# A SwiGLU block with Strassen's seven products for two of three token blocks, and the down projection in its own phase

## The chip, the cores and the metric

The kernel runs on one core of one Trainium2 chip. The metric is the device time of one execution in microseconds (us). PE is the matrix engine (PEld its weight loads), DVE the vector engine, ACT the scalar engine, POOL the GpSimd engine, SP the engine whose queue issues most transfers.

## The reference, cut to what matters

One decoder layer for 1024 prompt tokens and 32 sample tokens, in float32. The change touches the stretch from the memory attention's output projection to the end:

```python
x = layer_norm(DEEPNORM_ALPHA * x + memory_attention(x, mem_k, mem_v, w_mem_q, w_mem_o), ln2_g, ln2_b)
ffn = (jax.nn.silu(x @ w_gate) * (x @ w_up)) @ w_down      # w_gate, w_up 1024 x 2816, w_down 2816 x 1024
x = layer_norm(DEEPNORM_ALPHA * x + ffn, ln3_g, ln3_b)
```

## The kernel before

Activations lie with features on the 128 partitions and tokens along the free dimension, in three blocks of 384, 384 and 288 tokens (0, 1 and 2). Every float32 operand of PE is split in two rounded parts, high (a cast by ACT) and low (value minus high, by DVE). A product of a 128x128 weight tile and a block is three matmuls (`mm3`, L205 to L207): high by high, high weight by low value, low weight by high value.

Weights come as a stream of strips of 128x1024 (512 KB): a DMA issued from ACT's queue into `wraw` (two buffers), the cast to `whi` (L186), the subtraction to `wlo` (L187), four buffers of each. `gemm` goes through groups of four strips, inside them block by block; a strip is released behind block 2, which starts the split of a later one. All instructions are given out in program order, and a scheduler with a cost model decides the order in each engine's queue; every queue is then worked off strictly in that order.

The mem output projection (strips 50 to 57) adds its results to the residual `z` (L767, DVE) and sums the features on POOL (L777). Behind the last strip of a block its layer norm (`norm`) is put on a list and advanced step by step beside later products: a ones-matmul on PE sums over partitions (L788), ACT copies the mean (L791), the subtraction goes half to DVE and half to POOL (L796), ACT squares (L800) into the two `sq` buffers, DVE adds (L809 to L812), a second ones-matmul (L813), an inverse root (L443 to L446), a multiplication by DVE (L820), gain and bias feature by feature in turn on ACT and POOL (L826, L824), and the split of the result (L829, L830) into `a0h`, `a0l` (features 0 to 3) and `a1h`, `a1l` (4 to 7).

The feed-forward part takes the 22 feature tiles of the hidden dimension in chunks of 4 (the last of 2). A chunk is its gate and up strips, the gated values (`evac_gu`: silu by ACT L922, product by DVE L931, split L933 and L934) in SBUF, and the down strips. The last chunk goes block by block, so that the final norm of one block runs beside the products of the next; block 2's takes the short way (`fine`, L796 to L806).

Of the kernel before, what the change touches and what calls it, by code (L numbers as in the profile page):

```python
# [13 lines left out]
OP = mybir.AluOpType  # L14
# [28 lines left out]
def _weight_stream(i):  # L43
# [92 lines left out]
# ---------------------------------------------------------------- kernel  # L136
class Body:
# [4 lines left out]
    # ---- small helpers  # L142
# [66 lines left out]
    # groups: list of strip groups; x(b, k) -> (hi, lo) APs; evac(n, b, ps)  # L209
    def gemm(self, base, nstrips, x, evac, kt=8, blocks=(0, 1, 2), group=4):  # L210
# [26 lines left out]
    def body(self, st):  # L237
# [3 lines left out]
        self.limit = 50  # L241
# [15 lines left out]
    def phase12(self, st):  # L257
# [13 lines left out]
        self.s_x1 = scr("s_x1", [128, 8 * T])  # L271
        self.qs = self.t(self.cp, [128, 4, 32], "qs")
# [7 lines left out]
    def project(self, A, xa, og):  # L280
        tc, nc, a = self.tc, self.nc, self.a

        # queries: the tokens of each tile in the order of their residue mod 4
# [31 lines left out]
        with tc.tile_pool(name="ps_a", bufs=1, space=PSUM) as self.pp2, tc.tile_pool(name="ssm_small", bufs=1) as self.sp, tc.tile_pool(name="ssm_part", bufs=1) as sh, \  # L315
# [21 lines left out]
            # g_att and g_ssm: the factors that the sums of squares over 1024 instead of 512 and the doubled y leave  # L337
# [54 lines left out]
    def gemm_v(self, base, nch, lhs, rows, evac, release=True):  # L392
        # lhs(r, k) -> (hi, lo) stationary APs of row tile r
# [46 lines left out]
    # ---- -2/sqrt(ps + eps), ps [128, n] in PSUM  # L440
# [8 lines left out]
    # ---- sums of squares over features, for the rms norms  # L449
# [51 lines left out]
    # ---- residual and the recurrent half of the output projection  # L501
# [25 lines left out]
    # ---- windowed attention: prompt heads, with the sample batches as filler  # L527
# [22 lines left out]
    def attention(self):  # L550
# [7 lines left out]
        # a query tile meets its own and the previous key tile in full, and in the older ones the keys of its residue  # L558
        # mod 4 only; scores are laid out as [older tiles, 32 keys each | previous tile | own tile]
# [23 lines left out]
        def trans(h, qt):  # L583
# [13 lines left out]
            if qt and not e:  # L597
                # the key tile that is far from the odd tile of the pair only
# [3 lines left out]
        # two query tiles at a time; in the columns of a residue they meet the same older tiles  # L602
        def pv(hp, q0):
# [7 lines left out]
            # the own keys of the even tile are the previous ones of the odd tile  # L611
# [44 lines left out]
    # the first head pair, kept until its half of the mixer is free  # L656
# [12 lines left out]
    # ---- windowed attention of the sample batches, four at a time on the column groups of the array  # L669
# [93 lines left out]
    # ---- residual + layer norm of one block; z [128, 8, n] holds the residual and then the result  # L763
# [7 lines left out]
    # sums over the feature tiles: the first ones on GpSimd, those from cut on on VectorE  # L771
# [573 lines left out]
```

## Time and profile before

| | |
|---|---|
| time, three runs | 1746.70, 1746.38, 1744.56 us, median 1746.38 |
| span of the profiled execution | 1744.7 us, 1.7 us under the median of the runs |
| busy, share of the span | PE 94%, DVE 45%, ACT 29%, POOL 19% |

The span runs from the first to the last recorded instruction or transfer; what lies around it is the 1.7 us. A recorded matmul overlaps the next one, so PE's pitch is read from the starts of matmuls that follow each other. The granted clock stands as a share of full speed: 1.00 is 2.4 GHz and 0.5 is 1.2 GHz.

### The profile page before, as it was taken

To read this page: it belongs to the slowest core of one execution; us is meant where nothing else is said; L and a number is where in the kernel's file an instruction comes from. 1 tells how busy PE (TensorE), PEld (TensorE's weight loads), DVE (VectorE), ACT (ScalarE), POOL (GpSimd) and SP (SyncE) were. 2 spreads that over 40 slices of the span, in tenths; PEclk is the share of its full clock that TensorE was granted. 3 is DMA by queue.
4 is the path that set the end of the run, shared out by engine and by line. 5 is a ranking of instruction groups with operands and counts; after the bars stand their busy time and mean duration, and the time that the engine had idled before them with its cause. 6 is when DMAs were issued, how large, how long until landed. Compare 5 with 4: busy or idle time off the path is not lost.

```text
span 1744.7 us, 27141 instructions
## 1 busy us (share of the span) xinstructions
PE 1644.6 (94%) x11150; PEld 1505.1 (86%) x11150; DVE 793.4 (45%) x1614; ACT 506.5 (29%) x990; POOL 324.9 (19%) x372
## 2 busy tenths in 40 slices
PE   7797998999999988999998999999999999999996
PEld 7786785666766978987898999999999999999995
DVE  7564482177554985245427623223223322322347
ACT  5221121176334254245304520121121121121124
POOL 3403412032222644002126400000000000000025
PEclk9899999999999989999999999999999999999998
DMA  7435777813422366136610111111111111111102
GB/s 269 118 77 137 204 207 156 291 57 118 142 73 95 113 198 210 49 121 216 223 49 26 35 48 39 49 49 49 49 49 49 49 49 49 49 49 49 49 0 100
DMA packets 89052, 174.77 MB, mean 100 GB/s; under 512 B 12832, under 2 KB 48160, under 8 KB 88160
## 3 DMA queue, kind: packets, MB, share of 16 engines
q1 hardware_dynamic: 71072, 108.02, 20.6%
q10 hardware_dynamic: 17856, 65.02, 11.1%
q8 instruction: 88, 1.44, 0.3%
q14 instruction: 36, 0.29, 0.1%
HBM read 139.86 MB, written 33.14 MB: 99 GB/s over the span
## 4 chain that ended last, share of the span: by engine, by line
PE 79%; DVE 9%; DMA 5%; ACT 2%; SPq 2%; POOL 2%; issue 1%; ACTq 0%; POOLq 0%; DVEq 0%
PE g L205 21%; PE g L207 21%; PE g L206 21%; PE s L568 2%; PE s L570 2%; DVE wlo L187 1%; PE g L592 1%; PE q L743 1%; DMA wraw<-in_wst_dram 1%; POOL z L824 1%; DMA skv<-in_cv_dram 1%; DMA skv<-in_ckT_dram 1%; DVE z L820 1%; PE g L403 1%; PE g L404 1%
## 5 line engine op out<-in xcount | busy, mean ns | idle before, releaser
L205 PE MATMUL g<-a0h,whi 128*128 128x384 f32 (+1 forms) x1008 | 331.6, 331 | 12.4 <-ACT whi L186 7.6
L206 PE MATMUL g<-a0l,whi 128*128 128x384 f32 (+1 forms) x1008 | 330.0, 327 | 3.5 <-DVE a0l L830 3.5
L207 PE MATMUL g<-a0h,wlo 128*128 128x384 f32 (+1 forms) x1008 | 329.5, 327 | 2.3 <-DVE wlo L187 2.2
L205 PE MATMUL g<-a1h,whi 128*128 128x384 f32 (+1 forms) x960 | 312.2, 326 | 0.8 <-ACT a1h L328 0.8
L206 PE MATMUL g<-a1l,whi 128*128 128x384 f32 (+1 forms) x960 | 309.9, 323 | 2.0 <-DVE a1l L330 1.8
L207 PE MATMUL g<-a1h,wlo 128*128 128x384 f32 (+1 forms) x960 | 309.8, 323 | 0.0
L186 ACT CAST whi<-wraw 128x1024 fp32r<-128x1024 f32 x122 | 127.9, 1049 | 413.7 <-PE g L206 355.8
L187 DVE TENSOR_TENSOR wlo<-wraw,whi 128x1024 fp32r<-128x1024 f32 x122 | 162.6, 1334 | 117.0 <-ACT whi L186 116.8
L205 PEld LDWEIGHTS g<-a0h,whi 128*128 128x128 f32 x1008 | 192.5, 191 | 18.6 <-ACT whi L186 7.6
L206 PEld LDWEIGHTS g<-a0l,whi 128*128 128x128 f32 x1008 | 193.2, 192 | 5.6 <-DVE a0l L830 4.1
L207 PEld LDWEIGHTS g<-a0h,wlo 128*128 128x128 f32 x1008 | 193.1, 192 | 4.8 <-DVE wlo L187 3.3
L205 PEld LDWEIGHTS g<-a1h,whi 128*128 128x128 f32 x960 | 181.3, 189 | 6.1 <-issue 3.1
L206 PEld LDWEIGHTS g<-a1l,whi 128*128 128x128 f32 x960 | 181.4, 189 | 2.9 <-DVE a1l L330 2.0
L207 PEld LDWEIGHTS g<-a1h,wlo 128*128 128x128 f32 x960 | 181.5, 189 | 1.2 <-issue 1.1
L931 DVE TENSOR_TENSOR sil<-sil,g 128x384 f32<-128x384 f32 (+1 forms) x66 | 34.4, 521 | 268.6 <-PE g L207 266.8
L205 PE MATMUL g<-hh,whi 128*128 128x384 f32 (+1 forms) x480 | 154.2, 321 | 0.0
L206 PE MATMUL g<-hl,whi 128*128 128x384 f32 (+1 forms) x480 | 154.1, 321 | 0.0
L207 PE MATMUL g<-hh,wlo 128*128 128x384 f32 (+1 forms) x480 | 154.0, 321 | 0.0
L777 POOL TENSOR_TENSOR acc<-z 128x384 f32<-128x384 f32 (+1 forms) x9 | 9.8, 1085 | 738.0 <-DVE z L769 691.2
L769 DVE TENSOR_TENSOR z<-z,g 128x384 f32<-128x384 f32 (+1 forms) x120 | 61.4, 518 | 109.2 <-PE g L207 109.1
L207 PEld LDWEIGHTS g<-hh,wlo 128*128 128x128 f32 x480 | 90.2, 188 | 0.0
L206 PEld LDWEIGHTS g<-hl,whi 128*128 128x128 f32 x480 | 90.1, 188 | 0.0
(371 smaller groups left out, 2509.2 us busy)
## 6 DMA issues: line engine op xcount, KB each, us to landing
wraw<-in_wst_dram ACTq DMA_DIRECT2D x124, 512.0 KB, 3.4
skv<-in_ckT_dram SPq DMA_DIRECT2D x40, 256.0 KB, 4.5
skv<-in_cv_dram SPq DMA_DIRECT2D x40, 256.0 KB, 4.9
kvm<-in_cmk_dram SPq DMA_DIRECT2D x16, 512.0 KB, 5.0
wraw<-in_cmv_dram SPq DMA_DIRECT2D x16, 512.0 KB, 4.4
out_dram<-stg SPq DMA_DIRECT2D x32, 128.0 KB, 4.0
zt<-in_xT_dram SPq DMA_DIRECT2D x8, 384.0 KB, 3.5
s_z<-zt SPq DMA_DIRECT2D x8, 384.0 KB, 2.3
```

The source lines that it names most:

```text
L186: self.nc.scalar.copy(h[:], r[:])
L187: self.nc.vector.tensor_tensor(out=l[:], in0=r[:], in1=h[:], op=OP.subtract)
L205: mm(out, wh, xh, start=start, stop=False)
L206: mm(out, wh, xl, start=False, stop=False)
L207: mm(out, wl, xh, start=False, stop=stop)
L403: mm(ps[:, :256], xh, wh, start=k == 0, stop=False)
L404: mm(ps[:, :256], xh, wl, start=False, stop=False)
L568: mm(ps[:, 32 * nf:w], q, k[:, 128 * max(qt - 1, 0):128 * qt + 128], start=True, stop=True)
L570: mm(ps[32 * r:32 * r + 32, 0:32 * nf], q[:, 32 * r:32 * r + 32], k[:, 0:128 * nf].rearrange("p (i r) -> p r i", r=4)[:, r], start=True, s ...
L592: nc.tensor.transpose(ps[:, 128 * x:128 * x + 128], S[:, c:c + 128], self.ident[:])
L769: self.nc.vector.tensor_tensor(out=z[:, k], in0=z[:, k], in1=ps[:, :n], op=OP.add)
L931: v.tensor_tensor(out=hf[:, :n], in0=hf[:, :n], in1=ps[:, :n], op=OP.mult)
```

## The change

For blocks 0 and 1 the gate and up products of a feature tile are seen as a 2x2 product: weight halves a11, a12 (gate, input features 0 to 3 and 4 to 7) and a21, a22 (up), value halves b11, b21 (block 0) and b12, b22 (block 1). Instead of eight products of halves there are Strassen's seven, m1 to m7, each of 12 matmuls of 384 columns. Sums of values (`combine`) are formed once, behind the norms; sums of weights are formed for each feature tile on POOL. Nine half strips for each tile are split by ACT and DVE. Block 2 keeps direct products. The gated values go to DRAM (`s_h`) and come back in `down`, a phase of its own in chunks of 4, 4, 4, 4, 2 and 4. The mem output projection does strips 0 to 3 for blocks 0 and 1, strips 4 to 7 for all, and strips 0 to 3 once more, loaded and split again, for block 2. Strips of gate and up are loaded through SP's queue, the gate strip into `wraw`, the up strip into `wru` of a pool `up` that is opened where the pool `ln3` of the norms was closed.

```diff
-CHUNKS = [(0, 4), (4, 4), (8, 4), (12, 4), (16, 4), (20, 2)]
+NF = 22
+DOWN = [(0, 4), (4, 4), (8, 4), (12, 4), (16, 2), (18, 4)]
+MO, GU = 50, 58
+DN = GU + 2 * NF
...
-                    if b == 2:
+                    if b == rel:
                         self.release(base + s)
...
+        self.rows = list(range(MO + 8)) + list(range(MO, MO + 4)) + list(range(DN, a["wst"].shape[0]))
+        self.s_h = scr("s_h", [128, NF * T])
...
-        with tc.tile_pool(name="z2", bufs=1) as zp, tc.tile_pool(name="ln3", bufs=1) as self.lp, \
-                tc.tile_pool(name="ffn", bufs=1) as fp:
+        with tc.tile_pool(name="z2", bufs=1) as zp:
             z = self.load_z(zp, self.s_x1)
-            self.gemm_n(50, 8, xs, self.post_ln(z, x, 28, 36))
-            self.advance(99)
...
+            with tc.tile_pool(name="xc", bufs=1) as xp:
+                with tc.tile_pool(name="ln3", bufs=1) as self.lp:
+                    X = self.mem_out(z, xp, x, xs)
+                with tc.tile_pool(name="up", bufs=1) as up:
+                    self.gate_up(up, X, x[2])
+            with tc.tile_pool(name="ln4", bufs=1) as self.lp, tc.tile_pool(name="ffn", bufs=1) as fp:
+                self.down(z, fp)
...
+    def mem_out(self, z, xp, x, xs):
...
+            self.todo.append(self.norm(z[b], acc[b], 28, 36, x[b] if b == 2 else None))
+            if b == 0:
+                self.todo.append(self.combine(X, xp, z, ("m4", "m2")))
+            if b == 1:
+                self.todo.append(self.combine(X, xp, z, ("m3", "m5", "m1", "m6", "m7")))
+        X = {}
+        self.gemm_n(MO, 4, xs, lambda n, b, ps: evac(n, b, ps), blocks=(0, 1), rel=1)
+        self.gemm_n(MO + 4, 4, xs, lambda n, b, ps: evac(n + 4, b, ps))
+        self.gemm_n(MO + 8, 4, xs, lambda n, b, ps: evac(n, b, ps), blocks=(2,))
+        self.advance(99)
+        return X
...
+    def combine(self, X, xp, z, names):
+        nc = self.nc
+        part = lambda i: z[i % 2][:, 4 * (i // 2):4 * (i // 2) + 4]
+        b11, b12, b21, b22 = (part(i) for i in range(4))
+        recipe = {"m4": (b21, b11, OP.subtract, "a", 0), "m2": (b11, None, None, "a", 0),
+                  "m3": (b12, b22, OP.subtract, "a", 1), "m5": (b22, None, None, "a", 1),
+                  "m1": (b11, b22, OP.add, "1", 0), "m6": (b11, b12, OP.add, "6", 0), "m7": (b21, b22, OP.add, "7", 0)}
+        for n in names:
...
+                src = self.t(self.lp, [128, 4, 384], "sq", bufs=2)[:]
+                (nc.gpsimd if n in ("m6", "m7") else nc.vector).tensor_tensor(out=src, in0=p, in1=q, op=op)
...
+            nc.scalar.copy(hi[:], src)
+            nc.vector.tensor_tensor(out=lo[:], in0=src, in1=hi[:], op=OP.subtract)
...
+    def gate_up(self, up, X, x2):
...
+            raws[f] = [self.t(self.wp, [128, 1024], "wraw", bufs=2), self.t(up, [128, 1024], "wru", bufs=2)]
+            for i, r in enumerate(raws[f]):
+                nc.sync.dma_start(r[:], a["wst"][GU + 2 * f + i])
+        names = ("a22", "a11", "m2", "m5", "m1", "m6", "m7", "a12", "a21")
...
+                src = self.t(up, [128, 512], "wt", bufs=3)[:]
+                g.tensor_tensor(out=src, in0=q[p_], in1=q[q_], op=op)
+            t_ = self.t(self.wp, [128, 2, 512], "whi" if n in ("a22", "a11") else "wlo", F32R, 4)
+            act.copy(t_[:, 0], src)
+            v.tensor_tensor(out=t_[:, 1], in0=src, in1=t_[:, 0], op=OP.subtract)
...
+        raw(0)
+        for i in range(4):
+            unit(i)
...
+            product(p4, 384, U("a22"), *X["m4"])
+            act.copy(e4, p4[:, :384])
+            step()
+            product(p3, 384, U("a11"), *X["m3"])
+            act.copy(e3, p3[:, :384])
+            step()
+            product(p4, 384, U("m2"), *X["m2"], first=False)
+            g.tensor_tensor(out=e3, in0=e3, in1=e4, op=OP.add)
+            tt(out=d, in0=e3, in1=p4[:, :384], op=OP.subtract)
+            step()
+            product(p3, 384, U("m5"), *X["m5"], first=False)
+            tt(out=e3, in0=e3, in1=p3[:, :384], op=OP.subtract)
+            act.activation(s2, p3[:, :384], AF.Silu)
+            step()
...
+            product(p1, 384, U("m1"), *X["m1"])
+            act.copy(e1, p1[:, :384])
+            g.tensor_tensor(out=e1, in0=e1, in1=d, op=OP.add)
+            step()
+            product(p6, 384, U("m6"), *X["m6"])
+            tt(out=e1, in0=e1, in1=p6[:, :384], op=OP.add)
+            g.tensor_tensor(out=s2, in0=s2, in1=e1, op=OP.mult)
+            put(s2, f, 1)
+            step()
+            product(p1, 384, U("m7"), *X["m7"], first=False)
+            tt(out=e3, in0=e3, in1=p1[:, :384], op=OP.add)
+            act.activation(e3, e3, AF.Silu)
+            tt(out=e3, in0=e3, in1=p4[:, :384], op=OP.mult)
+            put(e3, f, 0)
+            step()
...
+            product(pg, n, U("a11"), *x2[0])
+            product(pg, n, U("a12"), *x2[1], first=False)
...
+            product(pu, n, U("a21"), *x2[0])
+            product(pu, n, U("a22"), *x2[1], first=False)
+            tt(out=sil[:, :n], in0=sil[:, :n], in1=pu[:, :n], op=OP.mult)
+            put(sil, f, 2)
...
+    def down(self, z, fp):
...
+                r = self.t(fp, [128, 4, 384], "hr", bufs=2)[:, :nf, :n]
+                nc.sync.dma_start(r, self.s_h[:, NF * off + f0 * n:NF * off + (f0 + nf) * n]
...
+                nc.scalar.copy(H[b][0], r)
+                nc.vector.tensor_tensor(out=H[b][1], in0=r, in1=H[b][0], op=OP.subtract)
...
+            for bs in ((0,), (1,), (2,)) if last else ((0, 1, 2),):
+                self.gemm_n(base, nf, lambda b, k: tuple(t_[:, k, :] for t_ in H[b]), evac_d, kt=nf, blocks=bs)
```

Line numbers move by 5 or 6 in the helpers (the norm's subtraction is L802, its multiplication L826); the new lines are L956 and L963, L964 (`combine`), L978 (strip loads), L995 to L998 (`unit`) and L1005 (`product`).

The order on DVE around the end of the mem output projection, before; z_1669 is block 1, sq_9705 holds block 2's squares, and `sil` and `hl` belong to the first feed-forward chunk:

```order
L820 TENSOR_TENSOR z_1669_8914<-z_1669_8914,rs_y_9603 128x1536 x2
L809 TENSOR_TENSOR sq_9705<-sq_9705 128x2x288
L931 TENSOR_TENSOR sil_9760<-sil_9760,g_9762 128x384
L809 TENSOR_TENSOR sq_9708<-sq_9708 128x2x288
L830 TENSOR_TENSOR a0l_1718_9524<-z_1669_8914,a0h_1717_9523 128x1536
L811 TENSOR_TENSOR sq_9705<-sq_9705,sq_9708 128x2x288
L931 TENSOR_TENSOR sil_9817<-sil_9817,g_9819 128x384
L934 TENSOR_TENSOR hl_1759_9788<-sil_9760,hh_1758_9787 128x384
L812 TENSOR_TENSOR sq_9705<-sq_9705 128x288
L934 TENSOR_TENSOR hl_1759_9788<-sil_9817,hh_1758_9787 128x384
L444 TENSOR_TENSOR rs_q_9716<-rs_y_9715 128x288
L445 SCALAR_TENSOR_TENSOR rs_q_9716<-s_9703,rs_q_9716 128x288
```

The same place after the change; z_1668 is block 0, x1, x6, x7, a0 and a1 are the operands of m1, m6, m7, m3 and m5, and sq_9724 holds block 2's squares:

```order
L826 TENSOR_TENSOR z_1669_8909<-z_1669_8909,rs_y_9494 128x1536 x2
L956 TENSOR_TENSOR sq_9543<-z_1669_8909 128x1536
L956 TENSOR_TENSOR sq_9584<-z_1668_8908,z_1669_8909 128x1536
L964 TENSOR_TENSOR a1l_1737_9581<-z_1669_8909,a1h_1736_9580 128x1536
L964 TENSOR_TENSOR a0l_1735_9577<-sq_9543,a0h_1734_9576 128x1536
L964 TENSOR_TENSOR x1l_9618<-sq_9584,x1h_9617 128x1536
L964 TENSOR_TENSOR x6l_9624<-sq_9621,x6h_9623 128x1536
L815 TENSOR_TENSOR sq_9724<-sq_9724 128x2x288
L964 TENSOR_TENSOR x7l_9657<-sq_9654,x7h_9656 128x1536
L815 TENSOR_TENSOR sq_9727<-sq_9727 128x2x288
L817 TENSOR_TENSOR sq_9724<-sq_9724,sq_9727 128x2x288
L818 TENSOR_TENSOR sq_9724<-sq_9724 128x288
```

Where work of the first chunk stood between the steps of block 2's norm, seven long subtractions and sums of `combine` now stand between block 1's multiplication and block 2's sums of squares.

PE after the change, at the end of the mem output projection (g_9687 is its last product, s_9722 the sum of block 2's squares, g_9782 the first Strassen product, m4):

```order
L209 MATMUL g_9687<-a1l_1322_7661,whi_9586 128x288
L210 MATMUL g_9687<-a1h_1321_7660,wlo_9587 128x288
L819 MATMUL s_9448<-sq_9450,ones_70 128x384
L794 MATMUL s_9718<-acc_9484,ones_70 128x288
L819 MATMUL s_9722<-sq_9724,ones_70 128x288
L1005 MATMUL g_9782<-a0h_1708_9383,whi_9766 128x384
L1005 MATMUL g_9782<-a0l_1709_9384,whi_9766 128x384
```

No product stands between the ones-matmuls and the first Strassen product.

SP's queue after the change, with the waits of each transfer, from the load of the residual on:

```order
L860 DMA z_1670_8910<-s_x_96 128x2304 [waits DMAHW7_49]
L978 DMA wraw_9758<-in_wst_dram 128x1024 [waits DMAHW3_49,DMAHW2_49,DMAHW4_49,DMAHW1_49,DMAHW6_49,DMAHW0_49,DVE_49]
L978 DMA wraw_9762<-in_wst_dram 128x1024 [waits DMAHW5_49,DMAHW3_49,DMAHW7_49,DMAHW1_49,DVE_49]
L978 DMA wru_9759<-in_wst_dram 128x1024 [waits DVE_49,Activation_49,Pool_49]
L978 DMA wru_9763<-in_wst_dram 128x1024
L978 DMA wraw_9895<-in_wst_dram 128x1024 [waits DMAHW0_49,DVE_49,Pool_49]
```

The first load of an up strip (`wru_9759`) waits for DVE, ACT and POOL, that is for the last users of the closed pool whose space it takes; block 2's multiplication, the last reader of `rs_y`, is among them. The third gate strip (`wraw_9895`) waits for readers of the first.

The end of DVE's queue before; z_1669 is block 1, z_1670 block 2, and L804, L805 are block 2's sums of squares:

```order
L820 TENSOR_TENSOR z_1669_8914<-z_1669_8914,rs_y_15673 128x768 x2
L796 TENSOR_TENSOR z_1670_8915<-z_1670_8915,s_15732 128x576 x4
L804 TENSOR_TENSOR sq_15737<-sq_15737 128x2x288
L805 TENSOR_TENSOR sq_15737<-sq_15737 128x288
L804 TENSOR_TENSOR sq_15742<-sq_15742 128x2x288
L805 TENSOR_TENSOR sq_15742<-sq_15742 128x288
L820 TENSOR_TENSOR z_1669_8914<-z_1669_8914,rs_y_15673 128x768 x2
L444 TENSOR_TENSOR rs_q_15753<-rs_y_15752 128x288
L445 SCALAR_TENSOR_TENSOR rs_q_15753<-s_15735,rs_q_15753 128x288
L446 SCALAR_TENSOR_TENSOR rs_y_15752<-rs_q_15753,rs_y_15752 128x288
L820 TENSOR_TENSOR z_1670_8915<-z_1670_8915,rs_y_15752 128x576 x4
```

And after:

```order
L802 TENSOR_TENSOR z_1670_8910<-z_1670_8910,s_16446 128x576 x4
L451 SCALAR_TENSOR_TENSOR rs_q_16350<-s_16306,rs_q_16350 128x384
L810 TENSOR_TENSOR sq_16451<-sq_16451 128x2x288
L452 SCALAR_TENSOR_TENSOR rs_y_16349<-rs_q_16350,rs_y_16349 128x384
L810 TENSOR_TENSOR sq_16456<-sq_16456 128x2x288
L811 TENSOR_TENSOR sq_16451<-sq_16451 128x288
L826 TENSOR_TENSOR z_1669_8909<-z_1669_8909,rs_y_16349 128x768 x4
L811 TENSOR_TENSOR sq_16456<-sq_16456 128x288
L450 TENSOR_TENSOR rs_q_16467<-rs_y_16466 128x288
L451 SCALAR_TENSOR_TENSOR rs_q_16467<-s_16449,rs_q_16467 128x288
L452 SCALAR_TENSOR_TENSOR rs_y_16466<-rs_q_16467,rs_y_16466 128x288
L826 TENSOR_TENSOR z_1670_8910<-z_1670_8910,rs_y_16466 128x576 x4
```

Two of block 1's multiplications stood ahead of block 2's sums and two behind them; now all four, and the last step of block 1's inverse root (L451, L452), stand ahead of the last sum of block 2 (`sq_16456`, L811).

## Rows read from the trace of the kernel before

**Rows 1.** First lines of the page: span, busy time of each engine.
```profile
span 1744.7 us, 27141 instructions
...
PE 1644.6 (94%) x11150; PEld 1505.1 (86%) x11150; DVE 793.4 (45%) x1614; ACT 506.5 (29%) x990; POOL 324.9 (19%) x372
```

**Rows 2.** Busy time of each engine in stretches of the span (start:end, length, then engines).
```profile
770.00:850.00 80.00, 71.91 (x637) 57.64 (x637) 46.29 (x180) 44.34 (x145) 18.84 (x40) 1.00 0.61 205
860.00:950.00 90.00, 86.09 (x534) 84.55 (x533) 39.83 (x46) 20.76 (x24) 35.40 (x26) 1.00 0.19 67
950.00:1000.00 50.00, 45.58 (x252) 44.14 (x251) 34.87 (x33) 24.91 (x34) 23.39 (x14) 0.93 0.07 22
1000.00:1700.00 700.00, 700.00 (x4356) 699.21 (x4355) 210.46 (x324) 121.67 (x185) 8.58 (x6) 1.00 0.14 46
...
1723.40:1744.70 21.30, 4.26 (x11) 1.62 (x9) 14.81 (x25) 8.32 (x13) 8.46 (x9) 0.62 0.33 129
```

**Rows 3.** Timeline of PE, one strip of the gate product, block 0.
```profile
1115.79 0.33 PE L205 MATMUL g<-a0h,whi 128*128 128x384 f32 x1
...
1117.87 0.33 PE L205 MATMUL g<-a1h,whi 128*128 128x384 f32 x1
```

**Rows 4.** Groups of DVE by line and shape, 860 to 1000 us.
```profile
L796 DVE TENSOR_TENSOR z<-z,s 128x1536 f32<-128x1536 f32 x2 | 3.5, 1748 | 1.7 <-ACT mean L791 1.7
L820 DVE TENSOR_TENSOR z<-z,rs_y 128x1152 f32<-128x1152 f32 x2 | 2.6, 1354 | 0.0
...
L809 DVE TENSOR_TENSOR sq<-sq 128x576 f32<-128x576 f32 x2 | 1.5, 750 | 0.0
...
L444 DVE TENSOR_TENSOR rs_q<-rs_y 128x288 f32<-128x288 f32 x1 | 0.5, 457 | 2.3 <-ACT rs_y L443 2.3
```

**Rows 5.** The same for POOL.
```profile
L796 POOL TENSOR_TENSOR z<-z,mean 128x1152 f32<-128x1152 f32 x1 | 2.7, 2690 | 5.0 <-ACT mean L791 5.0
L777 POOL TENSOR_TENSOR acc<-z 128x384 f32<-128x384 f32 x2 | 2.0, 1012 | 27.9 <-DVE z L767 27.9
L777 POOL TENSOR_TENSOR acc<-z 128x288 f32<-128x288 f32 x1 | 0.8, 802 | 5.2 <-DVE z L767 5.2
```

**Rows 6.** The same for ACT.
```profile
L829 ACT CAST a0h<-z 128x1536 fp32r<-128x1536 f32 x2 | 2.9, 1472 | 6.4 <-POOL z L824 6.4
...
L800 ACT ACTIVATE sq<-z 128x1152 f32<-128x1152 f32 x2 | 2.2, 1160 | 0.0
L933 ACT CAST hh<-sil 128x384 fp32r<-128x384 f32 x4 | 2.0, 507 | 1.3 <-DVE sil L931 1.3
```

**Rows 7.** Timeline of norms of blocks 0 and 1, three places.
```profile
918.62 1.00 POOL L777 TENSOR_TENSOR acc<-acc,z 128x384 f32<-128x384 f32 x1 [3.08 <-DVE z L767]
...
920.29 3.53 POOL L796 TENSOR_TENSOR z<-z,mean 128x1536 f32<-128x1536 f32 x1 [0.68 <-ACT mean L791]
...
942.70 3.58 POOL L824 TENSOR_SCALAR z<-z,vneg,vecs 128x384 f32<-128x384 f32 x4
...
952.97 4.20 POOL L830 TENSOR_TENSOR a1l<-z,a1h 128x1536 fp32r<-128x1536 f32 x1
...
953.75 4.50 DVE L187 TENSOR_TENSOR wlo<-wraw,whi 128x1024 fp32r<-128x1024 f32 x1
```

**Rows 8.** DMA issues of the page: size, median us from issue to landing.
```profile
wraw<-in_wst_dram ACTq DMA_DIRECT2D x124, 512.0 KB, 3.4
...
kvm<-in_cmk_dram SPq DMA_DIRECT2D x16, 512.0 KB, 5.0
...
s_x<-z SPq DMA_DIRECT2D x4, 768.0 KB, 5.0
```

**Rows 9.** Timeline of the last 21 us.
```profile
1731.95 0.46 DVE L805 TENSOR_TENSOR sq<-sq 128x288 f32<-128x288 f32 x1
1732.32 1.82 DVE L820 TENSOR_TENSOR z<-z,rs_y 128x768 f32<-128x768 f32 x2
...
1734.77 0.46 DVE L444 TENSOR_TENSOR rs_q<-rs_y 128x288 f32<-128x288 f32 x1 [0.63 <-ACT rs_y L443]
```

More of the change, by code (lines that the diff above doesn't have):

```diff
@@ L49, in _weight_stream @@
     g, u, d = _strips(i["w_gate"][0]), _strips(i["w_up"][0]), i["w_down"][0]
-    for f0, nf in CHUNKS:
-        for f in range(f0, f0 + nf):
-            out += [g[f:f + 1], u[f:f + 1]]
+    for f in range(NF):
+        out += [g[f:f + 1], u[f:f + 1]]
+    for f0, nf in DOWN:
         out.append(_pairs(d[f0 * 128:(f0 + nf) * 128]))
@@ new lines, in rest, with evac @@
+            with tc.tile_pool(name="xc", bufs=1) as xp:
[6 more added lines that the diff above has]
+    def mem_out(self, z, xp, x, xs):
+        acc, seen = [[], [], []], [[], [], []]
+        def evac(n, b, ps):
+            self.add_block(z[b], n, ps, True)
+            at = seen[b]
+            at.append(n)
+            if len(at) > 1:
+                if len(at) == 2:
+                    acc[b].append(self.t(self.lp, [128, 384], "acc", bufs=3)[:, :BLK[b][1]])
+                self.nc.gpsimd.tensor_tensor(out=acc[b][0], in0=z[b][:, at[0]] if len(at) == 2 else acc[b][0],
+                                             in1=z[b][:, n], op=OP.add)
+            if len(at) < 8:
+                self.advance(3)
+                return
+            if b == 2:
+                x[b] = self.blk_pair(b)
+            self.todo.append(self.norm(z[b], acc[b], 28, 36, x[b] if b == 2 else None))
[9 more added lines that the diff above has]
+        return X
@@ new lines, in down, with evac_d @@
+    def down(self, z, fp):
+        tc, nc, a = self.tc, self.nc, self.a
+        base = MO + 12
+        self.prefetch(999, 4)
+        for ci, (f0, nf) in enumerate(DOWN):
+            H, acc = {}, {}
+            last = ci == len(DOWN) - 1
+            for b, (off, n) in enumerate(BLK):
+                r = self.t(fp, [128, 4, 384], "hr", bufs=2)[:, :nf, :n]
+                nc.sync.dma_start(r, self.s_h[:, NF * off + f0 * n:NF * off + (f0 + nf) * n]
+                                  .rearrange("p (k n) -> p k n", n=n))
+                H[b] = [self.t(self.ap_, [128, 4, n], f"a{ci % 2}{p}{b}", F32R)[:, :nf] for p in "hl"]
+                nc.scalar.copy(H[b][0], r)
+                nc.vector.tensor_tensor(out=H[b][1], in0=r, in1=H[b][0], op=OP.subtract)
+            def evac_d(n, b, ps):
+                self.add_block(z[b], n, ps, ci == 0)
+                if not last:
+                    return
+                if n == 0:
+                    acc[b] = []
+                self.sum_block(z[b], n, acc[b], 5)
+                y = self.cols(a["yT"], b)
+                if n < 7:
+                    self.advance(2 if n < 6 or b < 2 else 0)
+                elif b < 2:
+                    self.todo.append(self.norm(z[b], acc[b], 44, 52, None, y))
+                else:
+                    nm = self.norm(z[b], acc[b], 44, 52, None, y, True)
+                    for _ in range(6):
+                        next(nm)
+                    with tc.issue_after(self.sub.ins):
+                        self.advance(99)
+                    self.todo.append(nm)
+            for bs in ((0,), (1,), (2,)) if last else ((0, 1, 2),):
+                self.gemm_n(base, nf, lambda b, k: tuple(t_[:, k, :] for t_ in H[b]), evac_d, kt=nf, blocks=bs)
+            base += nf
+        self.advance(99)
```

132 lines of the change are left out of this document (62 added, 70 removed).

## The prediction

> **What bounds the kernel now.** I read the page first: PE is busy 94% of a span of 1744.7 us [rows 1]. That is an average, so I then read the busy times by stretch [rows 2]. From 1000 to 1700 us, inside the feed-forward part, PE is busy all 700.00 us at clock 1.00, DVE 210.46, ACT 121.67 and POOL 8.58. There only the number of matmuls counts: work taken off PE is gained in full, and the other engines have room. The second thing to see is the border between the mem output projection and the feed-forward part: from 860 to 1000 us PE is idle only 3.91 + 4.42 = 8.33 us, because the norms run beside the products of the next stage. The third is the end: the last product ends at about 1723.4, and 21.3 us of norm follow.
>
> One execution stands 1.7 us above its span; with it the profiled one is at 1746.4, the median of the runs. All sums below are made against 1746.4. Under 0.2% (3.5 us) is about what a measurement of this kernel cannot tell from no change.
>
> **Removed from PE.** Twelve matmuls of 384 columns start 1117.87 - 1115.79 = 2.08 us apart, 0.1733 us each [rows 3]. A feature tile needs 7 x 12 = 84 of them instead of 8 x 12 = 96. 22 x 12 = 264 matmuls less are **-45.8 us**. The matmuls of block 2 (288 columns, by columns 0.13 us each, an estimate) and those of the down projection stay. A feature tile then lasts 84 x 0.1733 + 48 x 0.13 = 20.8 us on PE.
>
> **Added at the border.** Before, block 2's norm had the first gate and up products (of block 0, then 1) beside it. After, the order shows no product between the last one of the mem projection and m4, and the first up strip is loaded only when block 2's multiplications are through; m4 needs a22, which lies in that strip. So the whole remainder of the norms, all of block 1's `combine` and a transfer lie bare. I follow it from the end of the last product, in us, with prices from [rows 4 to 8] unless named:
> - addition of the last tile with its delay, about 0.7; POOL's sum 0.80; ones-matmul and copy of the mean 0.67 (919.62, where POOL's sum ends, to 920.29): 2.2. POOL's half of block 2's subtraction, 2.69: 4.9.
> - Block 1's two multiplications, 1.75 each (the 1748 of 1536 columns), can't run beside that half. The rows show it: a DVE subtraction of two SBUF operands begun at 953.75 beside a POOL subtraction of 952.97 to 957.17 took 4.50 [rows 7]. So 8.4. Gains and biases on POOL 3.58: 12.0.
> - Five operations of 1536 columns on DVE (m3, m1, and the low parts of m5, m3, m1), 5 x 1.75: 20.7.
> - m6 and m7 on POOL, 3.53 each; they need the two `sq` buffers, which m3 and m1 held until now: 27.8. The low part of m6, 1.75: 29.5.
> - Block 2's squares need those buffers in turn: square 1.16, cast of m7 1.47, low part of m7 1.75, second square 1.16: 35.1. Sums 0.75 + 0.75 + 0.46: 37.0.
> - Ones-matmul and inverse root on ACT, between the 0.67 above and the 2.4 from 1732.41 to 1734.77 [rows 9], I take 1.5; three steps of 0.46; two multiplications of 1.35: 42.6.
> - Transfer of 512 KB: 3.4 for a strip, 5.0 for a `kvm`, I take 4.2; cast of 512 columns, 0.61 by interpolation: 47.4.
>
> **+47.4 us.** If DVE and POOL could overlap freely, about 6 less; if the operations last as long as the delayed ones there and the transfer 5.0, about 6 more: 41 to 53.
>
> The Trainium skill ("SBUF — State Buffer", "SBUF: two separate sides") calls the port pair that VectorE and GpSimd share an exclusive lock, held for a whole instruction, when a VectorE operation has two SBUF inputs and the GpSimd one reads SBUF. The pair at 952.97 and 953.75 agrees. By the rule the sum is the 47.4, without it about 41; here I go by the row.
>
> **Given back there.** The 8.33 us of the old border fall away. The second pass over strips 0 to 3 has only 24 x 0.13 = 3.1 us of PE work for each strip of 512 KB, which lands in 3.4 [rows 8] and is then split; I charge 2 (0 to 5). **-6.3 us.**
>
> **Start of the feed-forward part.** PE has been idle over 40 us and starts at half clock. In 950 to 1000 the mean clock was 0.93 after waits like those, so 7 us at half, 3.5 lost [rows 2]. The units are also short: a sum of 512 columns on POOL is 1.29 us (between 1.01 for 384 and 2.69 for 1152 [rows 5]), a subtraction on DVE 0.69 (between 0.46 for 288 and 0.75 for 576 [rows 4]), and the two exclude each other. a22 and a11 cost 1.4; three sums and splits 5.9; then POOL turns to the low half of block 2's value (2.69); the sum for m6 is ready at about 12.0, where PE at full speed wants it at 10.5. 1.5 more: **+5 us** (3 to 12).
>
> **In each feature tile.** POOL has 5 x 1.29 + 3 x 1.01 = 9.5 us, DVE's two-operand subtractions are 9 x 0.69 = 6.2: together 15.7 of 20.8 even if they exclude each other. ACT has nine casts of 0.61 and six reads of PSUM of about 0.5: 8.5. The units are made four products (8.3 us) ahead. I charge nothing; the cover is 5 us for each tile, and if it is gone each us costs 22.
>
> **Hand-over to the down phase.** The first load (768 KB, 5.0 for `s_x`, the same size [rows 8]) waits for PE's last m7; behind it the order has some 34 matmuls of block 2, 4.5 us. Load 5.0, cast 1.47 and the low part 1.75 less what the high products cover (0.7) end 3 us after PE runs dry, and part of a restart at half clock comes on top: **+5 us** (1 to 9). Later loads have a whole chunk's time.
>
> **The end.** The last sum of block 2 stood right behind its neighbour at 1731.95, and two multiplications of block 1 lay in the wait behind it, 1732.32 to 1734.14, before DVE went on at 1734.77 [rows 9]. After, all four stand ahead of it, 4 x 0.91 = 3.6, and two steps of the inverse root beside them: **+4.5 us** (2 to 9).
>
> **Sum.** -45.8 + 47.4 - 6.3 + 5 + 5 + 4.5 = +9.8: 1756.2, so about **1756 us**.
>
> **The rivals.**
> - *A shorter border: faster.* It decides below 47.4 - 9.8 = 37.6 us. For it: ACT, DVE and POOL are all added up with little overlap, and a transfer may start earlier than I think. At 30 us the time is 1739. Against it: each step waits for the one ahead by data or by one of the two `sq` buffers, and even free overlap leaves 41.
> - *About equal.* Border 41 and the other terms near their lower ends (3 + 1 + 2): -45.8 + 41 - 6.3 + 6 = -5; half way to it, 1748.
> - *Units come late in every tile: slower still.* If exclusive use stretches the 15.7 of 20.8 by waits in DVE's and POOL's strict order (a sum stands behind an addition that waits for a product), 1 us a tile adds 22: 1778. For it: POOL goes from 8.58 us in 700 [rows 2] to nearly half its time, and a DVE subtraction behind a long POOL one took 4.50 [rows 7]. Against: 8.3 us of lead.
> - *The clock falls in every tile.* A short wait each tile would put PE at half clock again and again: half of what 950 to 1000 shows (4.42 idle, 3.5 lost) in each of 22 tiles is 87 us, or 1843. The Trainium skill ("TensorE: Matmul & The Clock Gate", "HAM oscillation — how this bites in real kernels") tells of kernels in which PE's wait in each loop step re-throttles it every time. Here 0.93 after 950 agrees, while 770 to 850 has PE idle 8.1 of 80 us at clock 1.00 [rows 2], in small pieces. It needs long waits in every tile, which the lead speaks against.
>
> **How the numbers follow.** Forecast as summed, slower by 3.5 to 19 us: 0.61, its own range 1750 to 1765. Shorter border, faster by over 3.5: 0.14. About equal: 0.13. Late units: 0.10. Falling clock: 0.02. Slower together 0.73. The range 1744 to 1775 takes in the equal case and the bounds of the border, and leaves out most of the faster case and the upper half of the late units, about 0.18.
>
> **What would show it.** Right: PE idle for some 47 us after the last mem product, the chain there going over POOL's m6 and m7, block 2's norm and the transfer of `wru`; PE solid with a pitch near 20.8 us a tile after the first; clock near 0.5 behind the two pauses; last product to end near 26 us. Wrong: an idle stretch under 38 us at the border; PE idle in each tile with the wait on `wlo` or `wt`; a clock under 1.00 in the middle of the gate and up phase; or a wait on the spilled values between chunks of the down phase.

## The result and the profile after

The change makes the kernel slower. Five runs gave a median of 1760.18 us (1753.63 to 1763.34) against 1746.38 of before (1741.85 to 1749.44); the ratio is 1.008, with a 95% interval of 1.0059 to 1.0100. The profiled execution took 1760.06 us, 1.9 above its span.

The first lines of its page, to be held against [rows 1]:

```profile
span 1758.2 us, 27853 instructions
...
PE 1612.3 (92%) x10886; PEld 1468.9 (84%) x10886; DVE 959.6 (55%) x1798; ACT 597.0 (34%) x1165; POOL 564.7 (32%) x548
```

PE is busy 32.3 us less, and the span is 13.5 us longer: PE waits about 46 us more. The busy times by stretch (columns as in [rows 2]) show where:

```profile
960.00:1001.00 41.00, 1.30 (x2) 0.50 (x2) 24.91 (x19) 17.59 (x19) 16.52 (x11) 0.50 0.07 26
1001.00:1022.00 21.00, 19.00 (x96) 18.74 (x97) 18.25 (x15) 9.23 (x17) 17.72 (x12) 0.86 0.11 29
1100.00:1400.00 300.00, 300.00 (x1889) 300.00 (x1889) 155.45 (x215) 109.30 (x215) 154.49 (x116) 1.00 0.24 78
1470.00:1480.00 10.00, 8.78 (x41) 8.27 (x42) 6.66 (x6) 4.42 (x4) 0.00 (x0) 0.83 0.84 281
1729.70:1758.20 28.50, 5.87 (x11) 2.47 (x10) 18.21 (x27) 9.01 (x14) 13.20 (x13) 0.57 0.31 119
```

In the middle of the gate and up phase (1100 to 1400) PE is busy all 300.00 us at clock 1.00, with DVE and POOL at about half. The losses lie at three places: the border (1.30 us of PE work in 41) with the restart behind it, the hand-over to the down phase and the end. The list of waits of PE from 860 us on names them (total, times, longest):

```profile
PE s L819 <- DVE sq L818: 39.1, 3, 35.1
PE g L1005 <- ACT whi L997: 9.7, 1, 9.7
PE s L812 <- DVE sq L811: 8.4, 2, 5.5
PE g L208 <- ACT a0h L1085: 3.3, 1, 3.3
PE g L1005 <- DVE wlo L998: 1.8, 1, 1.8
```

The timeline of PE at the border, with the idle time ahead of a row and what ended it in brackets:

```profile
951.83 0.29 PE L210 MATMUL g<-a1h,wlo 128*128 128x288 f32 x1
952.98 0.91 PE L819 MATMUL s<-sq,ones 128*128 128x384 f32 x2 [0.85 <-DVE sq L818]
...
990.13 1.30 PE L819 MATMUL s<-sq,ones 128*128 128x288 f32 x2 [35.10 <-DVE sq L818]
1001.16 0.69 PE L1005 MATMUL g<-a0h,whi 128*128 128x384 f32 x1 [9.73 <-ACT whi L997]
```

The last product of the mem projection ends at 952.13, the first Strassen product starts at 1001.16: 49.0 us, of which 35.10 and 9.73 are single waits. The chain of work there (start, duration, what):

```profile
958.49 1.34 DVE z L802
...
961.60 4.04 POOL z L830 x4
...
965.66 3.43 DVE sq L956 x2
...
972.57 4.80 POOL sq L956
...
978.90 3.48 DVE x6l L964
...
982.40 1.16 ACT sq L806
...
984.96 1.77 DVE x7l L964
...
993.48 1.37 DVE z L826
...
997.15 1.15 ACT a0h L835
```

The reader is to see that it passes through POOL's sum for m6 (4.80, where 3.53 had been shown at rest), the low part of m6 on DVE (3.48 for an operation of 1.75, because POOL's sum for m7 was running beside it), and only then reaches block 2's squares (982.40), which had to wait for the two `sq` buffers. Its last step is not the transfer alone: POOL's first sum of weights, which waits for the load, starts at 999.99, so the strip had landed; but in ACT's queue the first cast of weights (1000.50) stands behind the second cast of block 2's values (999.44, 1.15). Transfer and cast end within half a us of each other.

The end, PE's timeline:

```profile
1729.45 0.29 PE L210 MATMUL g<-a1h,wlo 128*128 128x288 f32 x1
1732.85 0.88 PE L819 MATMUL s<-sq,ones 128*128 128x384 f32 x2 [3.11 <-DVE sq L818]
1734.38 2.29 PE L794 MATMUL s<-acc,ones 128*128 128x288 f32 x4 [0.64 <-POOL acc L783]
1742.21 1.33 PE L812 MATMUL s<-sq,ones 128*128 128x288 f32 x2 [5.55 <-DVE sq L811]
```

From the last product (1729.74) to the end of the span are 28.5 us. Before they were 21.0: the 21.3 of [rows 2] are counted from 1723.40, and the last product ended at 1723.66. Block 2's mean (L794) is 4.6 us behind the last product; it was 0.3 before.

Executions of one kernel differ by several us ahead of the border: the same instructions bring block 2's second ones-matmul at the border (990.13 above) at 981.85 in one kernel below and at 989.13 in another. The same holds between before and after. The last matmul that both have in the same place of PE's order, first before, then after:

```profile
884.02 0.33 PE L207 MATMUL g<-a1h,wlo 128*128 128x384 f32 x1
888.33 0.33 PE L210 MATMUL g<-a1h,wlo 128*128 128x384 f32 x1
```

From there to the end of the span are 860.7 and 869.9 us, so of the 13.5 us between the spans 9.2 lie behind it and 4.3 ahead of it. For this reason the experiments are compared by the stretch from the last mem product to the end of the span, 806.1 us in the changed kernel (1758.2 - 952.13), and by single waits. In a kernel that differs only in its end the stretch ahead of that end still varied by some 2 us.

### The profile page after: what moved, and what is told of

The parts are those of the page before. It is cut to its first block, busy times and chain, and to the rows that moved or that the text cites. A ratio compares the mean times of both kernels' runs of the same rounds, so it can differ in the third digit from the quotient of the medians.

```text
span 1758.2 us, 27853 instructions
## 1 busy us (share of the span) xinstructions
PE 1612.3 (92%) x10886; PEld 1468.9 (84%) x10886; DVE 959.6 (55%) x1798; ACT 597.0 (34%) x1165; POOL 564.7 (32%) x548
## 4 chain that ended last, share of the span: by engine, by line
PE 76%; DVE 11%; DMA 6%; POOL 2%; ACT 2%; issue 2%; SPq 1%; ACTq 0%; POOLq 0%; DVEq 0%
PE g L1005 18%; PE g L208 12%; PE g L210 12%; PE g L209 12%; PE s L1005 8%; PE s L574 2%; PE s L576 2%; POOL z L830 1%; PE q L749 1%; PE g L598 1%; DVE z L826 1%; DVE wlo L190 1%; DMA skv<-in_ckT_dram 1%; DMA U<-s_u 1%; DMA skv<-in_cv_dram 1%
## 5 line engine op out<-in xcount | busy, mean ns | idle before, releaser
L208 PE MATMUL g<-a0h,whi 128*128 128x384 f32 (+1 forms) x720 | 238.9, 334 | 13.5 <-ACT whi L189 8.4
L210 PE MATMUL g<-a0h,wlo 128*128 128x384 f32 (+1 forms) x720 | 237.0, 329 | 1.2 <-DVE wlo L190 1.2
L208 PE MATMUL g<-a1h,whi 128*128 128x384 f32 (+1 forms) x720 | 237.1, 329 | 0.9 <-ACT a1h L334 0.9
L209 PE MATMUL g<-a0l,whi 128*128 128x384 f32 (+1 forms) x720 | 237.0, 329 | 0.3 <-DVE a0l L1086 0.3
L209 PE MATMUL g<-a1l,whi 128*128 128x384 f32 (+1 forms) x720 | 233.7, 325 | 1.8 <-DVE a1l L336 1.8
L210 PE MATMUL g<-a1h,wlo 128*128 128x384 f32 (+1 forms) x720 | 234.4, 326 | 0.0
L995 POOL TENSOR_TENSOR wt<-wraw,wru 128x512 f32<-128x512 f32 x44 | 57.8, 1313 | 147.6 <-DVE wlo L998 147.6
L1005 PE MATMUL g<-a0h,whi 128*128 128x384 f32 x352 | 95.0, 341 | 9.7 <-ACT whi L997 9.7
L997 ACT CAST wlo<-wt 128x512 fp32r<-128x512 f32 x110 | 66.2, 617 | 94.0 <-PE g L1005 83.0
L998 DVE TENSOR_TENSOR wlo<-wt,wlo 128x512 fp32r<-128x512 f32 x110 | 92.3, 854 | 3.2 <-ACT wlo L997 1.5
L1005 PE MATMUL g<-a1h,wlo 128*128 128x384 f32 x352 | 92.8, 334 | 0.0
```

The lines of the kernel that those rows point to most:

```text
L208: mm(out, wh, xh, start=start, stop=False)
L209: mm(out, wh, xl, start=False, stop=False)
L210: mm(out, wl, xh, start=False, stop=stop)
L995: g.tensor_tensor(out=src, in0=q[p_], in1=q[q_], op=op)
L997: act.copy(t_[:, 0], src)
L998: v.tensor_tensor(out=t_[:, 1], in0=src, in1=t_[:, 0], op=OP.subtract)
```

## The experiments

**The load of the first up strip.** The strips get space that does not hang on the norms:

```diff
-            with tc.tile_pool(name="xc", bufs=1) as xp:
+            with tc.tile_pool(name="xc", bufs=1) as xp, tc.tile_pool(name="wu", bufs=1) as self.up0:
...
-            raws[f] = [self.t(self.wp, [128, 1024], "wraw", bufs=2), self.t(up, [128, 1024], "wru", bufs=2)]
+            raws[f] = [self.t(self.wp, [128, 1024], "wraw", bufs=2), self.t(self.up0, [128, 1024], "wru", bufs=2)]
```

> The up strips get a pool of their own, opened ahead of the norms' pool, so the first load no longer waits for the norms' space; nothing else is changed. Theory (the border is a chain of waits, and the load is its last link): m4 and m3 run in the gap, m2 is the first product behind it and starts about where m4 starts now (1001 us), so about 8 us less: span 1758.2 - 8 = 1750 (1748 to 1753). Rival (the work of DVE and POOL there sets the length, the load only looks last): within 2 us of 1758.

Span 1752.5, time 1754.37; the stretch from the last mem product (951.67) is 800.8, 5.2 us shorter. PE's timeline:

```profile
955.41 0.91 PE L819 MATMUL s<-sq,ones 128*128 128x384 f32 x2 [2.00 <-DVE sq L818]
...
969.70 0.69 PE L1005 MATMUL g<-a0h,whi 128*128 128x384 f32 x1 [12.89 <-ACT a0h L963]
...
999.11 0.61 PE L1005 MATMUL s<-a0h,whi 128*128 128x288 f32 x1 [6.93 <-ACT a0h L835]
1001.50 0.61 PE L1005 MATMUL s<-a0l,whi 128*128 128x288 f32 x1 [1.78 <-DVE a0l L836]
```

m4 and m3 did move into the gap, but the next product in PE's queue was one of block 2 (`s`), which waits for ACT's and DVE's split of block 2 (6.93 and 1.78). And the splits of the first units, which now stood early in DVE's queue, held up block 1's last sums: its ones-matmul started 3.74 us behind the last product (955.41 less 951.67), 0.85 in the changed kernel. So the load is a link, worth about 5 us and not 8: the next wait stands right behind it, and what is moved ahead holds up others.

**m6 and m7 on DVE.**

```diff
-                (nc.gpsimd if n in ("m6", "m7") else nc.vector).tensor_tensor(out=src, in0=p, in1=q, op=op)
+                nc.vector.tensor_tensor(out=src, in0=p, in1=q, op=op)
```

> The sums for m6 and m7 are formed by DVE instead of POOL; nothing else is changed. Theory: they stand on the chain, and 4.79 + 3.42 on POOL with the 3.47 of m6's low part behind them become 3 x 1.75; the first Strassen product comes 6 to 7 us earlier, span 1751 (1749 to 1754). Rival (they lie beside the chain): no change, within 2 us of 1758.

Span 1746.3, time 1748.14; from the last mem product (944.72) 801.6, 4.5 us shorter. Of the 11.9 us between the spans some 7 lie ahead of the border, where nothing was changed; at the border itself:

```profile
976.77 1.30 PE L819 MATMUL s<-sq,ones 128*128 128x288 f32 x2 [29.16 <-DVE sq L818]
987.81 0.69 PE L1005 MATMUL g<-a0h,whi 128*128 128x384 f32 x1 [9.74 <-ACT whi L997]
```

The wait fell from 35.10 to 29.16, 5.9 us, the other stayed: the sums of m6 and m7 stood on the chain, at the size expected or a little under (6 to 7).

**The buffers.** The sums get a buffer of their own:

```diff
-                src = self.t(self.lp, [128, 4, 384], "sq", bufs=2)[:]
+                src = self.t(self.lp, [128, 4, 384], "cs")[:]
```

> The sums of values get one buffer of their own (cs) and no longer take the norm's two sq buffers; nothing else is changed. Theory (the sq buffers tie the norms to the sums: block 1's second square waits some 8 us for m4, block 2's squares wait for m6 and m7): block 2's norm ends over 15 us earlier, its wait for the sums of squares falls from 35 us to under 20; but one buffer makes m3, m1, m6 and m7 a chain of sum, cast and subtraction (2 x 5.0 + 2 x 6.7 = 23 us behind the norm of block 1), and the first load still waits for the closed pool, of which cs is now the last tile: border 49.0 less 2 to 6, span about 1754 at the same start of the border. Rival (the buffers are not what ties them): both waits as before.

Span 1747.8, time 1749.68; from the last mem product (944.41) 803.4, 2.7 us shorter, little more than that stretch varies by itself.

```profile
959.66 1.30 PE L819 MATMUL s<-sq,ones 128*128 128x288 f32 x2 [13.02 <-DVE sq L818]
992.18 0.69 PE L1005 MATMUL g<-a0h,whi 128*128 128x384 f32 x1 [31.22 <-ACT whi L997]
```

The wait for block 2's squares fell from 35.10 to 13.02, so the two `sq` buffers did tie its norm to the sums. The border as a whole is 47.8 us: the wait for the first weights grew from 9.73 to 31.22, since m7's sum, now last, holds the space that the up strip takes: its last reader, the low part of m7, ends at 987.63 in the timeline of DVE, and the first weights are cast at 991.51. A link of 22 us came off, and the next one gave all but 1.3 us back at the border.

**The price of PE's work.** m7 twice:

```diff
             product(p1, 384, U("m7"), *X["m7"], first=False)
+            product(p1, 384, U("m7"), *X["m7"], first=False)
```

> The product m7 is formed and added twice in each of 22 feature tiles, so the gated values of block 0 are other ones: 264 matmuls of 384 columns more. Theory (PE alone sets the pace inside the phase): +45.8, span 1804 (1802 to 1807). Rival (half strips come late in each tile): the added work fills idle time, less than +40.

Span 1797.4, time 1799.19. The first Strassen product starts at 998.12 and the first one of the down phase at 1511.33, behind 0.97 us of waiting: 512.2 us for the phase, against 1470.89 - 3.29 - 1001.16 = 466.4 in the changed kernel. +45.8 us for 264 matmuls, to the tenth what the prediction takes off PE for as many. The span grew less (39.2): the execution came to the border 3.0 us earlier, the wait at the hand-over was 2.3 shorter, the down phase 0.9 (the clock stays at 1.00 from 1510.35 to 1520) and the end 0.4.

**The room in a tile.** Each sum of weights twice on POOL:

```diff
                 g.tensor_tensor(out=src, in0=q[p_], in1=q[q_], op=op)
+                g.tensor_tensor(out=src, in0=q[p_], in1=q[q_], op=op)
```

> Each of the five sums of weights on POOL is formed twice, into the same tile; results unchanged. 5 x 1.29 = 6.5 us more on POOL in each tile: 9.5 + 6.5 = 16.0 of 20.96. Theory by the prediction's sum (POOL and DVE's two-operand subtractions exclude each other fully: 15.7 + 6.5 = 22.2 of 20.96): 1.2 us a tile over, +25 to 30 us, with PE waiting for low halves in most tiles. Rival (only each queue's own work counts, the overlap is looser than that): PE stays busy in the phase, under +5.

Span 1775.1, time 1776.96; the phase takes 1486.17 - 3.20 - 1000.18 = 482.8 us, 16.4 more, 0.74 a tile. The middle of it:

```profile
1100.00:1400.00 300.00, 293.10 (x1821) 287.87 (x1820) 172.48 (x205) 99.86 (x205) 237.05 (x180) 1.00 0.23 74
```

POOL is busy 237.05 of 300 us, not full, and PE is still idle 6.90. Neither theory gave this. In the same stretch DVE and POOL wait for each other (total, times, longest):

```profile
DVE ed L1038 <- POOL e L1037: 82.6, 14, 5.9
POOL wt L995 <- DVE wlo L999: 52.3, 40, 2.9
```

In each of 14 tiles DVE waits 5.9 us for an addition that stands in POOL's queue behind the doubled sums, and POOL waits for DVE to free the `wt` buffers. So the strict order of the two queues costs time, as the prediction's rival of late units had it; how much of the 0.74 us is that and how much mutual exclusion is not shown. The room was 6.5 - 0.74 = 5.8 us a tile, the 5 of the prediction roughly.

**The chunks of the end.**

```diff
-DOWN = [(0, 4), (4, 4), (8, 4), (12, 4), (16, 2), (18, 4)]
+DOWN = [(0, 4), (4, 4), (8, 4), (12, 4), (16, 4), (20, 2)]
```

> The chunks of the down phase are 4, 4, 4, 4, 4, 2 as in the kernel before instead of 4, 4, 4, 4, 2, 4. Theory (what hides the norm of block 1 is the stretch of products behind it; in the last chunk block 2 has 12.8 us of products now and 6.4 with two strips): the end grows by about 6 us, span 1764 (1762 to 1768). Rival (the longer end comes with the other split of the chunks): the end goes back to 21 us, span 1751.

Span 1770.8, time 1772.86; the last product ends at 1729.62, the end is 41.2 us. PE's timeline:

```profile
1729.33 0.29 PE L210 MATMUL g<-a1h,wlo 128*128 128x288 f32 x1
1730.82 0.88 PE L819 MATMUL s<-sq,ones 128*128 128x384 f32 x2 [1.20 <-DVE sq L818]
...
1745.81 1.62 PE L819 MATMUL s<-sq,ones 128*128 128x384 f32 x2 [12.81 <-DVE sq L818]
```

Block 0's second ones-matmul is now behind the last product, and block 1's follows 15 us later. The sign is the theory's, the size twice it (12.7 for 6): both norms slip; block 1's stretch is half as long too, which the theory left out.

**Block 2's products twice at the end.** In the last chunk the loop over the features goes around twice for block 2:

```diff
-                        for k in range(kt):
+                        for k in list(range(kt)) * times:
...
-                self.gemm_n(base, nf, lambda b, k: tuple(t_[:, k, :] for t_ in H[b]), evac_d, kt=nf, blocks=bs)
+                self.gemm_n(base, nf, lambda b, k: tuple(t_[:, k, :] for t_ in H[b]), evac_d, kt=nf, blocks=bs,
+                            times=2 if bs == (2,) else 1)
```

> In the last chunk of the down phase block 2's products are formed twice (the second pass starts the sum anew, so results are unchanged): 96 matmuls of 288 columns, 12.8 us, more in front of the end. Theory (the end grew because block 1's norm has only 12.8 us of products beside it): with 25.6 us it is through before the last product; the stretch from the last product to the end falls from 28.5 to 21 (20 to 23), span 1758.2 + 12.8 - 7.5 = 1763.5 at the same start of the border. Rival (the order of the last steps on DVE and POOL sets it, whatever stands beside block 1's norm): the end stays at 28, span 1771.

Span 1757.5, time 1759.33:

```profile
1738.21 0.29 PE L210 MATMUL g<-a1h,wlo 128*128 128x288 f32 x1
1738.34 0.65 PE L794 MATMUL s<-acc,ones 128*128 128x288 f32 x2
1739.55 0.75 PE L794 MATMUL s<-acc,ones 128*128 128x288 f32 x2 [0.56 <-DVE acc L783]
1744.37 2.49 PE L812 MATMUL s<-sq,ones 128*128 128x288 f32 x4 [4.07 <-DVE sq L811]
```

The last product ends at 1738.50, the end is 19.0 us, 9.5 shorter and even 2.0 under that of before. So the end depends on the products beside block 1's norm. The kernel before had more of them: in its last chunk block 2 had its gate, up and down products, 144 matmuls or 19.2 us, between these two rows of its timeline:

```profile
1702.33 0.29 PE L205 MATMUL g<-a0h,whi 128*128 128x288 f32 x1
...
1723.37 0.29 PE L207 MATMUL g<-hh,dl 128*128 128x288 f32 x1
```

The down phase of its own took the gate and up products (12.8 us) away from there, and four strips in place of two gave 6.4 back. With 6.4, 12.8, 19.2 (before) and 25.6 us of block 2's products the end is 41.2, 28.5, 21.0 and 19.0 us.

**The order of the last sums.**

```diff
-                    self.advance(2 if n < 6 or b < 2 else 0)
+                    self.advance(2 if b < 2 else n < 5)
```

> In the last chunk block 1's norm is advanced more slowly beside block 2 (one step for each result, not two), so that in DVE's queue its four multiplications stand behind the last sum of block 2's squares; they still stand ahead of its inverse root. Theory: of the 7.2 us by which the end grew, 3.5 is these four ahead of the last sum (1742.08 to 1745.64) and the rest is that block 2's mean waits on PE behind block 1's second sum; so the end falls from 28.5 to 25 (24.5 to 27), the wait for that sum stays. Rival (the multiplications lie in a wait anyway): within 1 us of 28.5.

Span 1751.3, time 1753.12; the last product ends at 1723.58, the end is 27.7 us, 0.7 shorter: the rival was right. The chain of work at the end shows why:

```profile
1735.63 0.74 DVE sq L811 x2
1736.37 3.49 DVE z L826 x4
...
1739.94 0.51 ACT rs_y L449
```

The last sum (1735.63) no longer waits for the four multiplications, but ACT's inverse root (1739.94) does: in ACT's queue stand three of the features that they feed. The 3.5 us only moved.

**Another order of the border.** Block 2 goes first through the mem projection, and its direct products of the first ten feature tiles are PE's work while block 1's norm and the sums of values are made; those tiles are loaded again for Strassen's products. The kernel also forms the sums of m6 and m7 on DVE, gives the up strips a space of their own (as in two experiments above) and reads strips 0 to 3 once:

```diff
-        self.gemm_n(MO, 4, xs, lambda n, b, ps: evac(n, b, ps), blocks=(0, 1), rel=1)
-        self.gemm_n(MO + 4, 4, xs, lambda n, b, ps: evac(n + 4, b, ps))
-        self.gemm_n(MO + 8, 4, xs, lambda n, b, ps: evac(n, b, ps), blocks=(2,))
-        self.advance(99)
+        self.gemm_n(MO, 8, xs, evac, blocks=(2, 0, 1), rel=1)
...
+                    G = self.gate_up(X, x[2])
+                    next(G)
+                    self.advance(99)
...
+        for f in range(K):
+            direct(f, step2)
+        up = yield
+        seq = [(f, n) for f in range(NF) for n in names if f >= K or n not in ("a12", "a21")]
```

> Another order: in the mem projection block 2 comes first, then 0 and 1, and strips 0 to 3 are read once; block 2's gate and up products of the first 10 feature tiles (10 x 6.4 = 64 us) run while block 1's norm and the sums of values are made; then Strassen tiles, the first 10 without block 2; m6 and m7 summed by DVE; strips of these 10 tiles are loaded and split twice. Theory (the 49 us are lack of other products beside a chain, and any product that needs nothing of it fills them): PE's idle time at the border falls below 20 us, 25 to 35 us less than after: 1728 (1722 to 1736), faster than before. Rival (DVE, ACT and POOL are the limit there, more splits beside them lengthen the chain as much as they cover): over 1745.

Six runs: median 1732.13 us, ratio to before 0.9926 (0.9910 to 0.9941). PE's waits from 860 us on:

```profile
PE s L819 <- DVE sq L818: 18.1, 3, 8.1
PE s L812 <- DVE sq L811: 8.4, 2, 5.6
```

Of the 44.8 us of single waits at the border 15.0 are left (6.87 at 958.79 and 8.08 at 989.42), ones-matmuls that stand in PE's queue ahead of their sums.

**The same with later ones-matmuls.**

```diff
             if len(at) < 8:
-                self.advance(3)
+                self.advance(2)
```

> As v1_block2_first, but beside the mem projection the pending norms are advanced two steps for each result, not three, so the ones-matmul of a norm (the sum of squares) is put later in PE's queue. Theory (what is left of the border in v1 are ones-matmuls that stand in PE's queue before their sums are ready, 18.1 us in three waits): these waits fall below 10, 5 to 9 us less than v1: 1725 (1721 to 1730). Rival (the norm is what is late, not its place in the queue): within 3 us of v1's 1732.

Six runs: median 1729.82 us, ratio to before 0.9911 (0.9886 to 0.9936).

```profile
PE s L819 <- DVE sq L818: 10.7, 2, 6.9
```

The waits for sums of squares fell from 18.1 to 10.7, of which 3.78 belong to the end; so 6.87 of the 15.0 are left at the border. From the last mem product it is 4.4 us shorter than the first new order in the profiled executions (774.0 for 778.4), but their spans are equal (1730.2 and 1730.3), and the medians differ by 2.3, inside their scatter. Both beat the kernel before, and so Strassen's products do in this order; the gain of the second over the first is not settled. This order without Strassen's products was not run; at the old border it had the 8.3 us of waits and 3.5 of clock to win, so the share of the order alone is open.

## Why the prediction was right

It gave 1756 us and the sign, and the time lies in its own range (1750 to 1765). Its steps one by one:

- **Removed, -45.8.** Right; m7 twice gave +45.8 back.
- **The border, +47.4.** 49.0 measured, 3 of it ones-matmuls, for which the sum gives nothing back though PE had them before too. The links and their order were those of the sum up to the last step, where ACT's casts of block 2 stand beside the transfer. Three links were moved in experiments: m6 and m7 (5.9), the load (5.2) and the buffers (22.1 off one wait, 1.3 off the border). DVE's operations of two SBUF operands wait for POOL's, as the sum took it: the low part of m6, begun at 978.90 while POOL's sums ran to 980.75, took 3.48 for 1.75. The Trainium skill ("SBUF — State Buffer", "SBUF: two separate sides") calls the port pair that the two share an exclusive lock, held for a whole instruction; this pair agrees. In the steady tiles the runs leave open how far the two engines exclude each other: 1.2 us over the pitch on the sum's reckoning cost 0.74, and the order of the queues had a part in it.
- **Given back, -6.3.** The mem projection's weights cost 1.9 us of waits (0.95, 0.36, 0.58) for the 2 charged: -6.4. But the old border also had its restart at a lower clock. The prediction reads 3.5 us lost from it in [rows 2] and takes that as the price of the new start, without giving the old one back. With it the term is -9.9.
- **The start, +5.** The phase takes 466.4 us, and 22 tiles of 84 x 0.1733 + 48 x 0.1333 are 461.1: 5.3, of which 2.9 are the clock (0.86 in the mean of 21 us) and 1.8 a wait for a low half.
- **Nothing in each tile.** Right, PE 300.00 of 300.
- **Hand-over, +5.** Right: PE is idle 3.3, and the down phase lasts 258.9 us to its last product where 176 x (6 x 0.1733 + 3 x 0.1333) = 253.4 would do. Of these 5.4 five pairs of ones-matmuls of the last norms take 3.2 (0.64 each by the starts around them), and the kernel before has such pairs in its last chunk too. The other 2.2 are the restart (clock 0.83 in the mean of the 10 us from 1470, 1.7 us) and a wait of 0.33 for a low part. 5.5 in all.
- **The end, +4.5.** 7.4 measured, and the step that failed is its cause. The prediction charged the four multiplications ahead of the last sum; moving them gave 0.7. What counts is that the norms of blocks 0 and 1 are late, because the change left 12.8 us of block 2's products beside the last of them in place of 19.2. POOL's sums for block 2's mean (1729.84 to 1734.32) stand behind block 1's subtraction (1722.93) and block 0's gains (1726.45). With 12.8 us more of products the end fell to 19.0. That the size still lay inside the stated 2 to 9 is luck.

The measured terms make -45.8 + 49.0 - 3 - 9.9 + 5.3 + 5.5 + 7.4 = +8.5, against the 9.2 us behind the last matmul in common. The medians lie 13.8 apart; that the rest of this is scatter ahead of the border fits the 4.3 us there, but is not shown run by run. The forecast of 9.8 came so near in part by luck: it left out two things to be given back (3 and 3.5), and it charged the border 1.6 and the end 2.9 too little.

Of the rivals, "a shorter border" fell with the 49.0 us, "about equal" with the ratio's interval, "late units" and "falling clock" with the full 300. The border could be shortened all the same, by giving PE other work: single links gave 1 to 6 us each at the border, the new order 28 from the last mem product on (806.1 to 778.4). The new order has two of those links in it as well, and no run has it without them.

## What to carry to other kernels

A saving in a phase whose engine is always busy was worth its matmuls to the tenth here; what it cost lay at the phase's two ends. A phase that is split off also takes its products away from whatever they used to hide, here the last norms. Before a phase is made to need everything that the phase ahead makes, ask what the bound engine does meanwhile: here 46 us were saved and 49 lost, and putting independent products (block 2's) into the gap turned a loss of 14 us into a gain of 13 to 15. Taking one link out of a serial chain shows the next one: compare the whole stretch, not the wait that went.

## What was not expected of the hardware

In the middle of the gate and up phase of the changed kernel, two groups of the same DVE subtraction of 512 columns stand side by side by line and shape (count, busy time, mean ns):

```profile
L998 DVE TENSOR_TENSOR whi<-wraw,whi 128x512 fp32r<-128x512 f32 x14 | 19.7, 1410 | 0.0
...
L998 DVE TENSOR_TENSOR whi<-wru,whi 128x512 fp32r<-128x512 f32 x14 | 9.7, 692 | 19.0 <-ACT whi L997 19.0
```

In each of these 14 tiles one half strip is subtracted while POOL forms a sum, and takes twice as long. PE does not feel it there; with five more sums on POOL in each tile (POOL at 79%) the pitch grew by 0.74 us of 21. I had expected either none or some 1.2; how much of the 0.74 comes from this overlap is open.

The same instructions ahead of the border took up to 8 us more or less from one execution to another (the last mem product ended at 943.87 in one and at 952.13 in another), more than most of the effects measured here. Spans alone would have misled: m6 and m7 on DVE seemed to give 11.9 us and gave 5.9 at the border, 4.5 to the end of the span.
